# Output projection's convolution rows as a step of their own, and one operand for the convolution norm's colsums

## The chip, the cores and the metric

The kernel runs on one core of a Trainium2 chip. The metric is device time in microseconds of one execution; the time before is the median of three runs. A profiled execution of its own gives the trace from which the rows below are read.

## The reference

One inference step of a two-layer decoder, for a prompt of 512 tokens and 8 sample tokens, which the kernel carries as 520 columns. Everything is fp32.

```
for each of 2 layers:
    x += 0.5 * SwiGLU_1(rmsnorm(x))              # 1024 -> 2816 -> 1024
    z  = rmsnorm(x) @ w_in                       # q,k,v,gate of 4 retention heads; q,k,v of 4 attention heads; 2 x 256 conv
    o_r = rmsnorm(retention(...)) * silu(gate)   # 512 rows
    o_a = sliding-window attention with sinks    # 256 rows
    u   = a * sigmoid(g)                         # 256 channels
    y   = depthwise_conv(u, 31 taps) + b
    o_c = silu(layer_norm(y)) @ pw               # 256 rows
    x += concat(o_r, o_a, o_c) @ w_out           # 1024 rows in, 1024 out
    x += 0.5 * SwiGLU_2(rmsnorm(x))
```

layer_norm takes the mean over the 256 channels, subtracts it, and divides by the root of the mean square of what is left.

## The kernel before, in words

Activations lie with channels on the partitions and the 520 columns along the free dimension: `x` is 8 blocks of 128 channels. Each fp32 operand is split into a high and a low part (`xh`, `xl`; for weights `wh`, `wl`), and `mm3` makes a product of 128 by 128 weights with 520 columns from three pairs of parts, in two halves of 260 columns: six matmuls. Weights come from HBM in chunks of eight such blocks (512 KB), four raw buffers deep. A chunk is split by ScalarE (`split_hi`, the high part) and VectorE (`split_lo`, the low part) into one of three buffers each; a split can only begin when the last matmul on the chunk three before it is done.

Between the two FFNs of a layer lies the mix stage. Its steps are generators, and each `yield` ends a piece of a step. `ORDER`, written out by hand, names the step of which the next piece is issued; each engine then runs its own instructions in that order. The names that matter here:

- `h` and `l` are the next chunk's high and low split; the high split runs on ScalarE (L290), the low one on VectorE (L296).
- `cv` is what follows the convolution's taps (`conv_rest`): a sum over 256 channels by a matmul with a constant matrix (`colsum`, L361), the mean subtracted (L726), the square (L728), another colsum, the reciprocal root, the silu, the split, the product with `pw`, and the split of the result.
- `n0` to `n3` are the retention heads' norms: square (L1140), colsum, three ScalarE and three VectorE instructions. `g0` to `g3` multiply by the gate and split into `xh` and `xl` (L1163 to L1168).
- `s0` to `s3` are the attention of 128 prompt tokens each: scores (L852), row maximum with bias (L837, VectorE), exponentials (L864, ScalarE), reciprocal sum, scaling (L873, ScalarE), transposes (L879), their copy from PSUM (L884, ScalarE), product with the values (L891), its high cast (L899, ScalarE) and low part (L901, VectorE). `sa` is the same for the sample tokens (scores L919).
- `AQ`, `AK`, `AV`, `RG` and others are the input projection's blocks of 128 rows with what follows each; `rs0`, `rs1` update the sample state (L1024, L1026).
- `a0` to `a7` and `b0` to `b7` are the output projection: `a` multiplies the four retention rows of w_out (24 matmuls) for one block of 128 output channels and adds the result to x (L1184); `b` does the same for two attention and two convolution rows (24 matmuls), and after its add issues `prep` for the next FFN: `xh` (L385, ScalarE), `xl` (L387, VectorE), the square (L392), and the sum of squares (`acc`, L395).

PSUM is four tiles of two banks each. A tile is free again when its last reader in the written order is done. Scratch rows (`wt`) rotate through six buffers. The next FFN's first hidden step begins right after `b7`, takes two PSUM tiles at once (gate and up, alternating), reads all eight blocks of `xh` and `xl`, and at its end issues the norm's colsum from `acc`.

Of the kernel before, what the change touches and what calls it, by code (L numbers as in the profile page):

```python
# [87 lines left out]

ORDER = """
CG0 al nrm h nrm pw l nrm pw h nrm l nrm CG0 rd RK0 CG0 CA0 h RK0 l CA1 CA0 h CG0 t l t t t CG1 t h t l t t t t CA1 t  # L90
RV1 h CG1 t CG1 l t t t t RV2 h t t RV1 l t t t t RV3 t RV1 h t RV2 l t t t t t RK1 h l t RV3 RV2 t ts ts RV1 RK1 t h
l RV2 RV1 RK1 RK1 RV2 RQ0 RK1 CG1 t t t t RQ0 t t h t l t t t t RQ1 RV3 RV0 h RQ1 qr l t t t t t RG0 t h t RV0 l t t t
RG0 t t RV0 AQ0 h t RG0 l t t t t AQ1 h AQ0 l t t RV0 h RV3 AQ1 RV3 RV0 t ri2 t AQ1 rv ri0 rv AQ1 RK0 cv ri0 AQ0 AQ0
rl AK0 AQ1 cv ri2 AQ1 rs0 cv RK0 rs0 AQ1 l h rs1 AV0 l rs1 AK0 AK0 RG1 h AK0 AV0 l AV0 rm RG1 h RG1 l AQ0 rm rm cv AQ0
RG2 AQ0 cv qs cv RG3 h RG2 cv l RG2 cv h RG3 AV0 RG3 cv AV0 RK0 kv cv kv cv kv AK0 l AK0 ri2 AK0 AK0 ri0 ri2 s1 ri0 n0
n2 s1 n1 n0 n3 s0 n3 n2 s0 n0 n1 n0 s3 s1 g0 n2 s1 n1 n2 g0 s1 n1 g2 n3 g1 s1 g1 g0 n3 g3 s0 s1 sa s2 g2 s3 g1 g3 s3
s1 s1 g2 g3 s0 s0 s1 sa a0 s3 s3 s2 a1 sa a0 s2 sa a2 a1 h s2 s2 l s3 a2 a3 s3 sa s3 a3 h sa s0 l s3 sa s0 s3 s0 sa s0
s2 a4 s0 s2 a5 a4 a6 a5 sa h s2 a6 a7 s2 s2 b0 l h l b1 b0 b0 b1 b0 b0 b2 h b0 b1 b1 b2 b1 b2 b1 b2 b3 l b4 h b3 b3 l
b2 b3 b5 b4 b3 b2 b4 b3 b4 b6 h b5 b5 l b4 b5 b7 a7 b6 b5 b4 b5 b6 b6 b7 b6 b7 b6 b7 b7 b7
""".split()  # L100


# [1 line left out]
START = "x0 h0 x1 s0 s1 h1 x2 x3 s2 h2 x4 s3 x5 s4 h3 x6 s5 x7 s6 s7 c2".split()  # L104


OUT = dict(a=("R0", "R1", "R2", "R3"), b=("A0", "A1", "C0", "C1"))


def ffn_steps():  # L110
# [14 lines left out]
def streams():  # L125

    w_in = [n for i, n in enumerate(ORDER) if len(n) == 3 and n[:2].isupper() and n not in ORDER[:i]]
    w_out = [(r, int(n[1])) for i, n in enumerate(ORDER) if n[0] in OUT and n[1:].isdigit() and n not in ORDER[:i] for r in OUT[n[0]]]
    return w_in, w_out
# [7 lines left out]
def step_kernel(ctx: ExitStack, tc: tile.TileContext, io: dict):  # L137
    nc = tc.nc
# [25 lines left out]
    ones = {}  # L164
# [13 lines left out]
    def prm(l, name, i=0, n=1):  # L178
        o = P_OFF[name] + i
        return par[:, l, o : o + n]  # L180
# [3 lines left out]
    def v2(t):  # L184
        return t.rearrange("p (a b) -> p a b", a=2)

    def unit(dt=F32):
        return units.tile([128, UNIT], dt, tag="m", name="m")
# [150 lines left out]
    def mm3(o, w, vh, vl, first, last):  # L339
        for i, (a, b) in enumerate(((w[0], vl), (w[0], vh), (w[1], vh))):  # L340
            for s in range(2):
                nc.tensor.matmul(  # L342
                    o[:, s, :HN], lhsT=a, rhs=b[:, s * HN : (s + 1) * HN],
                    start=first and i == 0, stop=last and i == 2,
                )
# [3 lines left out]
    def table(name):  # L349
        if act[0] != name:  # L350
            nc.scalar.preload_act_table_set(name)
            act[0] = name
# [5 lines left out]
    def colsum(o, w, parts):  # L358
        for i, v in enumerate(parts):
            for s in range(2):  # L360
                nc.tensor.matmul(  # L361
                    o[:, s, :HN], lhsT=w, rhs=v[:, s * HN : (s + 1) * HN],
                    start=i == 0, stop=i == len(parts) - 1,
                )
# [5 lines left out]
    def rsqrt(out, o):  # L370

        m = o[:, :, :HN]
        y0, t = wt("y0"), wt("nt")
        table(LNEXP)
        nc.scalar.activation(v2(y0), m, AF.Ln, bias=epst)
        nc.scalar.activation(y0, y0, AF.Exp, scale=-0.5)
        nc.scalar.activation(t, y0, AF.Square, scale=math.sqrt(0.5))
        yield
        nc.vector.scalar_tensor_tensor(v2(t), m, epst[:, :1], v2(t), op0=ALU.add, op1=ALU.mult)
        nc.vector.scalar_tensor_tensor(out, t, 1.5, y0, op0=ALU.subtract, op1=ALU.mult, reverse0=True)  # L380
# [221 lines left out]
    def mix(l, after):  # L602
# [5 lines left out]
        qs = su[:, 48:80].rearrange("p (a b e) -> p a b e", a=2, e=2)  # L608
# [5 lines left out]
        def two(t):  # L614
            return t[:, :UNIT].rearrange("p (c t) -> p c t", c=2)
# [102 lines left out]

        def conv_rest():
            y = conv["y"]  # L720
            o = ptile()
            colsum(o, ones[256], [y[:, 0], y[:, 1]])
            yield
            yc = two(unit())
            for c in range(2):
                nc.vector.tensor_sub(v2(yc[:, c]), v2(y[:, c]), o[:, :, :HN])  # L726
            yield
            nc.scalar.activation(y, yc, AF.Square)  # L728
            yield
            o = ptile()  # L730
            colsum(o, ones[256], [y[:, 0], y[:, 1]])
            yield
            r = wt("lnr")
            yield from rsqrt(r, o)
            for c in range(2):
                nc.vector.tensor_mul(y[:, c], yc[:, c], r)
            yield
            hi, lo = two(unit(F32R)), two(unit(F32R))
            table(SILU)
            for c in range(2):  # L740
                nc.scalar.activation(
                    y[:, c], y[:, c], AF.Silu, scale=prm(l, "ln_g", c), bias=prm(l, "ln_b", c)
                )
                nc.scalar.copy(hi[:, c], y[:, c])
            yield
            for c in range(2):
                nc.vector.tensor_sub(lo[:, c], y[:, c], hi[:, c].bitcast(F32))
            yield
            os = []
            for m in range(2):  # L750
                o = ptile()
                os.append(o)
                for k in range(2):
                    s = slice(k * 256 + m * 128, k * 256 + m * 128 + 128)
                    mm3(o, (pw[0][:, s], pw[1][:, s]), hi[:, k], lo[:, k], k == 0, k == 1)
            yield
            hl = two(unit(F32R)), two(unit(F32R))
            for m, o in enumerate(os):
                nc.scalar.copy(v2(hl[0][:, m]), o[:, :, :HN])
            yield  # L760
            for m, o in enumerate(os):
                nc.vector.tensor_sub(v2(hl[1][:, m]), o[:, :, :HN], v2(hl[0][:, m]).bitcast(F32))
            conv["o"] = hl
            yield
# [299 lines left out]
        def ret_sample_q():  # L1064
            for e in range(2):
                s = slice(64 * e, 64 * e + 64)
                nc.scalar.copy(qs[s, :, :, e], ret["q"][s, :, SEQ:])
            yield
# [103 lines left out]
        def row_input(name):  # L1172
            j = int(name[1])
            if name[0] == "R":
                return ret["hl", j]
            h_, l_ = (att if name[0] == "A" else conv)["o"]
            return h_[:, j], l_[:, j]

        def out(names, m, last):
            o = ptile()  # L1180
            for i, n in enumerate(names):
                mm3(o, next_tile(False), *row_input(n), i == 0, i == len(names) - 1)
            yield
            nc.vector.tensor_add(v2(x[:, m]), v2(x[:, m]), o[:, :, :HN])  # L1184
            yield
            if last:
                yield from after(m)

        def chunk_hi():
            while True:  # L1190
                split_hi()
                yield

        def chunk_lo():
            while True:
                split_lo(1)
                yield

        steps = dict(
            h=chunk_hi(), l=chunk_lo(), nrm=norm(), pw=pw_split(), rd=decayed(), ts=token_scales(), t=conv_taps(),  # L1200
            cv=conv_rest(), al=att_load(), AK0=att_qk(None), AV0=att_v(), qs=att_sample_q(), qr=ret_sample_q(), sa=att_sample(),
            rv=ret_vs(), rl=ret_load(), kv=ret_kv(), rm=ret_sample(), ri0=ret_prompt(0), ri2=ret_prompt(2),
        )
        for i in range(KD):
            steps.update({n + str(i): out(rows, i, n == max(OUT)) for n, rows in OUT.items()})
        for i in range(4):
            steps.update({
                f"RV{i}": ret_v(i), f"RG{i}": ret_gate(i), f"n{i}": ret_norm(i), f"g{i}": ret_out(i),
# [87 lines left out]
def host_arrays(i):  # L1296
# [83 lines left out]
    y=(KD, 128, NT), o_retp=(DEPTH, 4, 64, 128), o_rets=(DEPTH, 2, 128, 1024), o_kp=(DEPTH, 128, 128),  # L1380
# [38 lines left out]
```

## Time and profile before

| | us |
|---|---|
| median of 3 runs | 1912.63 |
| lowest and highest | 1911.82 to 1913.17 |
| the profiled execution's time | 1916.64 |
| its span in the trace | 1914.9 |
| TensorE busy | 1843.5 (96%) |
| VectorE busy | 1565.0 (82%) |
| ScalarE busy | 991.9 (52%) |

The span runs from the first instruction to the last; the execution's time has 1.7 us more around it. Busy is the time in which an engine had an instruction under way. Matmuls overlap each other, so an engine that is busy is not at its peak. In the rows below PE is TensorE, PEld its weight loads, DVE VectorE, ACT ScalarE and SP the engine that issues the loads.

### The profile page before, as it was taken

To read this page: it belongs to the slowest core of one execution; us is meant where nothing else is said; L and a number is where in the kernel's file an instruction comes from. 1 tells how busy PE (TensorE), PEld (TensorE's weight loads), DVE (VectorE), ACT (ScalarE), POOL (GpSimd) and SP (SyncE) were. 2 spreads that over 40 slices of the span, in tenths; PEclk is the share of its full clock that TensorE was granted. 3 is DMA by queue.
4 is the path that set the end of the run, shared out by engine and by line. 5 is a ranking of instruction groups with operands and counts; after the bars stand their busy time and mean duration, and the time that the engine had idled before them with its cause. 6 is when DMAs were issued, how large, how long until landed. Compare 5 with 4: busy or idle time off the path is not lost.

```text
span 1914.9 us, 37060 instructions
## 1 busy us (share of the span) xinstructions
PE 1843.5 (96%) x15182; PEld 1818.6 (95%) x15182; DVE 1565.0 (82%) x2691; ACT 991.9 (52%) x1844; POOL 23.3 (1%) x52
## 2 busy tenths in 40 slices
PE   8999999999989999999999999999998999999998
PEld 8999999999989999999999999999998999999998
DVE  8988898688667989888778988976886579889984
ACT  6545555433765645545455455545237555455452
POOL 0000000000100000000000000000000000000000
PEclk9999999999999999999999999999999999999999
DMA  5233333433313222333333332434332132333332
GB/s 181 77 101 100 89 100 111 138 108 114 117 35 97 79 89 89 90 110 98 112 88 90 91 97 89 123 110 127 100 114 102 45 98 69 100 107 92 93 96 89
DMA packets 54170, 189.35 MB, mean 99 GB/s; under 512 B 6272, under 2 KB 7152, under 8 KB 54000
## 3 DMA queue, kind: packets, MB, share of 16 engines
q1 hardware_dynamic: 50784, 177.35, 30.4%
q0 software_dynamic: 3072, 9.53, 1.5%
q8 instruction: 119, 1.95, 0.4%
q14 instruction: 51, 0.42, 0.1%
q10 hardware_dynamic: 144, 0.11, 0.0%
HBM read 179.50 MB, written 7.45 MB: 98 GB/s over the span
## 4 chain that ended last, share of the span: by engine, by line
PE 61%; DVE 26%; ACT 5%; DMA 4%; issue 4%; SPq 0%; DVEq 0%; ACTq 0%; POOL 0%; POOLq 0%
PE o L342 32%; PE o L334 27%; DVE wl L296 5%; DMA w<-in_w 3%; DVE wh L296 3%; DVE m L474 2%; DVE u L430 2%; DVE m L502 1%; DVE w L260 1%; DVE Rd L263 1%; ACT t L428 1%; DVE t L557 1%; DVE t L556 1%; DVE t L561 1%; DVE u L556 1%
## 5 line engine op out<-in xcount | busy, mean ns | idle before, releaser
L342 PE MATMUL o<-xl,wh 128*128 128x260 f32 x1920 | 389.3, 284 | 6.6 <-DVE xl L387 6.1
L342 PE MATMUL o<-xh,wl 128*128 128x260 f32 x1920 | 387.1, 283 | 1.1 <-DVE wl L296 1.1
L342 PE MATMUL o<-xh,wh 128*128 128x260 f32 x1920 | 386.9, 283 | 0.0
L334 PE MATMUL o<-m,wh 128*128 128x260 f32 x2592 | 350.5, 285 | 23.0 <-DVE t L443 11.3
L334 PE MATMUL o<-m,wl 128*128 128x260 f32 x2592 | 351.7, 285 | 21.3 <-DVE t L443 9.8
L290 ACT CAST wh<-w 128x1024 fp32r<-128x1024 f32 (+1 forms) x318 | 261.1, 821 | 200.8 <-PE o L342 127.7
L334 PEld LDWEIGHTS o<-m,wh 128*128 128x128 f32 x2592 | 327.4, 189 | 27.3 <-issue 12.3
L334 PEld LDWEIGHTS o<-m,wl 128*128 128x128 f32 x2592 | 328.5, 190 | 25.7 <-issue 10.8
L342 PEld LDWEIGHTS o<-xl,wh 128*128 128x128 f32 x1920 | 296.9, 189 | 7.9 <-ACT wh L355 6.1
L342 PEld LDWEIGHTS o<-xh,wl 128*128 128x128 f32 x1920 | 296.6, 189 | 1.3 <-DVE wl L296 1.3
L342 PEld LDWEIGHTS o<-xh,wh 128*128 128x128 f32 x1920 | 296.1, 189 | 0.0
L296 DVE TENSOR_TENSOR wl<-w,wh 128x1024 fp32r<-128x1024 f32 x150 | 183.3, 1222 | 36.1 <-ACT wh L290 32.7
L342 PE MATMUL o<-m,wh 128*128 128x260 f32 x1024 | 164.5, 282 | 4.1 <-DVE m L510 4.1
L342 PEld LDWEIGHTS o<-m,wh 128*128 128x128 f32 x1024 | 140.0, 188 | 5.0 <-DVE m L510 5.0
L290 ACT CAST wl<-w 128x512 fp32r<-128x512 f32 x168 | 103.9, 619 | 35.3 <-PE o L334 21.6
L290 ACT CAST wh<-Rd 128x512 fp32r<-128x512 f32 x126 | 78.3, 621 | 82.5 <-PE o L334 34.5
L290 ACT CAST wl<-Rd 128x512 fp32r<-128x512 f32 x126 | 78.3, 622 | 80.2 <-PE o L334 34.4
L428 ACT ACTIVATE t<-t 128x520 f32<-128x520 f32 x88 | 56.1, 638 | 122.8 <-DVE t L561 103.8
L334 PE MATMUL o<-xh,wh 128*128 128x260 f32 x624 | 115.4, 282 | 0.0
L334 PE MATMUL o<-xh,wl 128*128 128x260 f32 x624 | 115.4, 282 | 0.0
L296 DVE TENSOR_TENSOR wl<-w,wl 128x512 fp32r<-128x512 f32 x168 | 114.9, 684 | 0.0
L296 DVE TENSOR_TENSOR wh<-w,wh 128x512 fp32r<-128x512 f32 x168 | 114.9, 684 | 0.0
(216 smaller groups left out, 2660.0 us busy)
## 6 DMA issues: line engine op xcount, KB each, us to landing
w<-in_w SPq DMA_DIRECT2D x318, 512.0 KB, 3.6
out_y<-x SPq DMA_DIRECT2D x8, 260.0 KB, 2.0
m<-in_cm POOLq DMA_DIRECT2D x4, 512.0 KB, 4.3
m<-in_s_ret SPq DMA_DIRECT2D x4, 512.0 KB, 5.2
m<-sc POOLq DMA_DIRECT2D x8, 256.0 KB, 4.6
out_o_rets<-m POOLq DMA_DIRECT2D x4, 512.0 KB, 3.4
x<-in_x SPq DMA_DIRECT2D x3, 520.0 KB, 6.8
w<-in_w SPq DMA_DIRECT2D x4, 256.0 KB, 5.2
```

The lines of the kernel that those rows point to most:

```text
L260: nc.vector.tensor_sub(a21, a21, a11)
L263: nc.vector.tensor_sub(Rd[:, 0, :PC], a12, Rd[:, 1, :PC])
L290: nc.scalar.copy(spl[u][0], source(u))
L296: nc.vector.tensor_sub(lo, source(u), h.bitcast(F32))
L334: nc.tensor.matmul(o, lhsT=a[:, s], rhs=b, start=first and j == 0 and i == 0, stop=j == JP - 1 and i == 2, skip_group_check=True,)
L342: nc.tensor.matmul(o[:, s, :HN], lhsT=a, rhs=b[:, s * HN : (s + 1) * HN], start=first and i == 0, stop=last and i == 2,)
L428: nc.scalar.activation(t, t, AF.Silu)
L430: nc.vector.tensor_mul(u, u, t)
L474: nc.vector.tensor_sub(tl[:, c], src, th[:, c].bitcast(F32))
L502: nc.vector.tensor_sub(lo, a, h.bitcast(F32))
L556: nc.vector.tensor_add(d[:, HN:], c, v)
L557: nc.vector.tensor_mul(d[:, HN:], d[:, HN:], R[:, HN:])
```

## The change

The output projection is cut into three steps instead of two: `b` keeps the two attention rows, and a new step `c` multiplies the two convolution rows (12 matmuls) and adds its own result to x. `prep` still follows b's add. `c0` stands in the order behind the scores of s1; `c1` to `c4` stand around the softmax of s1, and `c5` to `c7` behind the sample attention's scores. The eight a steps keep their place, b keeps its place with half of its matmuls. Since w_out's blocks are stored in the order of first use, the two chunks with the convolution's rows now come first, and the h and l pieces from the 22nd on (h21 is the first of them) stand elsewhere. In `conv_rest` each colsum gets one operand, the sum of y's two blocks, made by an added VectorE instruction, in place of two operands that TensorE summed.

```diff
 (ORDER, from the retention's last pieces on)
-... kv cv kv cv kv AK0 l AK0 ri2 AK0 AK0 ri0 ri2 s1 ri0 n0
-n2 s1 n1 n0 n3 s0 n3 n2 s0 n0 n1 n0 s3 s1 g0 n2 s1 n1 n2 g0 s1 n1 g2 n3 g1 s1 g1 g0 n3 g3 s0 s1 sa s2 g2 s3 g1 g3 s3
-s1 s1 g2 g3 s0 s0 s1 sa a0 s3 s3 s2 a1 sa a0 s2 sa a2 a1 h s2 s2 l s3 a2 a3 s3 sa s3 a3 h sa s0 l s3 sa s0 s3 s0 sa s0
-s2 a4 s0 s2 a5 a4 a6 a5 sa h s2 a6 a7 s2 s2 b0 l h l b1 b0 b0 b1 b0 b0 b2 h b0 b1 b1 b2 b1 b2 b1 b2 b3 l b4 h b3 b3 l
-b2 b3 b5 b4 b3 b2 b4 b3 b4 b6 h b5 b5 l b4 b5 b7 a7 b6 b5 b4 b5 b6 b6 b7 b6 b7 b6 b7 b7 b7
+... kv cv kv cv kv AK0 l AK0 ri2 AK0 AK0 ri0 ri2 s1 c0 c0 ri0
+n0 n2 s1 n1 n0 n3 s0 n3 n2 s0 n0 n1 n0 s3 s1 g0 n2 s1 n1 n2 g0 c1 c1 s1 n1 c2 c2 g2 c3 c3 n3 h c4 c4 g1 l s1 g1 g0 n3
+g3 s0 s1 sa c5 c5 c6 c6 c7 c7 h s2 l g2 s3 g1 g3 s3 s1 s1 g2 g3 s0 s0 s1 sa a0 s3 s3 s2 a1 h sa a0 s2 l sa a2 a1 s2 s2
+s3 a2 a3 h s3 sa s3 l a3 sa s0 s3 sa s0 s3 s0 sa s0 s2 a4 s0 s2 a5 h a4 a6 a5 l sa s2 a6 a7 h s2 s2 b0 l b1 b0 b0 b1 b0
+b0 b2 b0 b1 b1 b2 b1 b2 b1 b2 b3 h b4 b3 b3 l b2 b3 b5 b4 b3 b2 b4 b3 b4 b6 b5 b5 b4 b5 b7 a7 b6 b5 b4 b5 b6 b6 b7 b6
+b7 b6 b7 b7 b7

-OUT = dict(a=("R0", "R1", "R2", "R3"), b=("A0", "A1", "C0", "C1"))
+OUT = dict(a=("R0", "R1", "R2", "R3"), b=("A0", "A1"), c=("C0", "C1"))

         def conv_rest():
             y = conv["y"]
-            o = ptile()
-            colsum(o, ones[256], [y[:, 0], y[:, 1]])
+            ys = wt("ys")
+            nc.vector.tensor_add(ys, y[:, 0], y[:, 1])
+            o = ptile()
+            colsum(o, ones[256], [ys])
             yield
...
             nc.scalar.activation(y, yc, AF.Square)
-            yield
-            o = ptile()
-            colsum(o, ones[256], [y[:, 0], y[:, 1]])
+            ys = wt("ys")
+            nc.vector.tensor_add(ys, y[:, 0], y[:, 1])
+            yield
+            o = ptile()
+            colsum(o, ones[256], [ys])
             yield
...
-            steps.update({n + str(i): out(rows, i, n == max(OUT)) for n, rows in OUT.items()})
+            steps.update({n + str(i): out(rows, i, n == "b") for n, rows in OUT.items()})
```

## Rows read from the trace of the kernel before

**Rows 1.** The page's part on busy time: us, share of the span, instructions.

```profile
PE 1843.5 (96%) x15182; PEld 1818.6 (95%) x15182; DVE 1565.0 (82%) x2691; ACT 991.9 (52%) x1844; POOL 23.3 (1%) x52
```

**Rows 2.** TensorE's waits over the span: total us, times, longest.

```profile
PE o L334 <- DVE t L443: 21.0, 12, 2.5
...
PE o L879 <- ACT m L873: 9.3, 2, 4.6
...
PE o L361 <- ACT rsq L1140: 1.8, 2, 0.9
PE o L342 <- DVE wl L296: 1.1, 1, 1.1
```

**Rows 3.** Windows of layer 0's chain: us, each engine's busy time, granted clock, DMA share.

```profile
528.00:530.00 2.00, 0.00 (x0) 0.00 (x0) 1.29 (x4) 1.94 (x4) 0.00 (x0) 1.00 0.00 0
...
534.00:536.00 2.00, 2.00 (x11) 1.41 (x10) 2.00 (x5) 1.94 (x4) 0.00 (x0) 0.50 0.03 8
```

**Rows 4.** Timeline of layer 0's chain: start, us, engine, line, operation, idle before.

```profile
529.66 0.76 DVE L379 SCALAR_TENSOR_TENSOR nt<-o,epst,nt 128x520 f32<-128x520 f32 x1 [0.67 <-ACT nt L377]
...
532.52 1.97 PE L879 MATMUL o<-cc,m 128*128 128x128 f32 x8 [4.63 <-ACT m L873]
534.42 3.62 PE L919 MATMUL o<-m 128*32 128x128 f32 x16
...
540.59 0.51 PE L342 MATMUL o<-xl,wh 128*128 128x260 f32 x2 [0.40 <-DVE st L837]
```

**Rows 5.** The chain that ended last, two pieces of layer 0's mix stage.

```profile
478.27 11.54 PE o L342 x96
...
568.10 37.40 PE o L342 x312
```

**Rows 6.** Groups by line and shape (busy us, mean ns), and one timeline row of two adds.

```profile
L296 DVE TENSOR_TENSOR wl<-w,wh 128x1024 fp32r<-128x1024 f32 x150 | 183.3, 1222 | 36.1 <-ACT wh L290 32.7
...
L387 DVE SCALAR_TENSOR_TENSOR xl<-x,par,xh 128x520 fp32r<-128x520 f32 x48 | 36.3, 758 | 20.7 <-ACT xh L385 20.7
...
L395 DVE TENSOR_TENSOR acc<-acc,sq 128x520 f32<-128x520 f32 x42 | 29.2, 695 | 0.7 <-ACT sq L392 0.2
...
L1184 DVE TENSOR_TENSOR x<-x,o 128x520 f32<-128x520 f32 x32 | 22.0, 693 | 25.7 <-PE o L342 25.5
...
591.08 1.30 DVE L1184 TENSOR_TENSOR x<-x,o 128x520 f32<-128x520 f32 x2
```

**Rows 7.** Timeline of layer 0 around cv's two colsums, by engine.

```profile
469.57 2.02 PE L361 MATMUL o<-m,one 128*128 128x260 f32 x8
...
493.64 3.66 PE L361 MATMUL o<-m,one 128*128 128x260 f32 x8
...
471.28 0.16 DVE L964 TENSOR_TENSOR su<-m,R 128x8 f32<-128x8 f32 x1
...
478.03 1.23 DVE L1024 SCALAR_TENSOR_TENSOR m<-m,su 128x1024 f32<-128x1024 f32 x1 [2.13 <-DMA m<-sc]
...
482.69 1.22 DVE L296 TENSOR_TENSOR wl<-w,wh 128x1024 fp32r<-128x1024 f32 x1
...
479.81 1.06 ACT L728 ACTIVATE m<-m 128x1040 f32<-128x1040 f32 x1
```

**Rows 8.** Timeline of layer 0's a steps, ScalarE, VectorE and TensorE.

```profile
550.91 0.99 ACT L884 COPY m<-o 128x1024 f32<-128x1024 f32 x1
553.09 1.06 ACT L290 CAST wh<-w 128x1024 fp32r<-128x1024 f32 x1 [1.19 <-PE o L342]
...
568.14 0.37 ACT L899 CAST m<-o 128x256 fp32r<-128x256 f32 x1 [3.14 <-PE o L891]
570.97 1.05 ACT L290 CAST wh<-w 128x1024 fp32r<-128x1024 f32 x1 [2.45 <-PE o L342]
...
568.54 0.42 DVE L901 TENSOR_TENSOR m<-o,m 128x256 fp32r<-128x256 f32 x1 [0.78 <-ACT m L899]
...
553.39 1.14 PE L891 MATMUL o<-m 128*64 128x128 f32 x16
```

More of the change, by code (lines that the diff above doesn't have):

```diff
@@ L90 @@
 CG0 al nrm h nrm pw l nrm pw h nrm l nrm CG0 rd RK0 CG0 CA0 h RK0 l CA1 CA0 h CG0 t l t t t CG1 t h t l t t t t CA1 t
[L91 to L94, printed above, removed]
@@ L95 @@
-RG2 AQ0 cv qs cv RG3 h RG2 cv l RG2 cv h RG3 AV0 RG3 cv AV0 RK0 kv cv kv cv kv AK0 l AK0 ri2 AK0 AK0 ri0 ri2 s1 ri0 n0
-n2 s1 n1 n0 n3 s0 n3 n2 s0 n0 n1 n0 s3 s1 g0 n2 s1 n1 n2 g0 s1 n1 g2 n3 g1 s1 g1 g0 n3 g3 s0 s1 sa s2 g2 s3 g1 g3 s3
-s1 s1 g2 g3 s0 s0 s1 sa a0 s3 s3 s2 a1 sa a0 s2 sa a2 a1 h s2 s2 l s3 a2 a3 s3 sa s3 a3 h sa s0 l s3 sa s0 s3 s0 sa s0
-s2 a4 s0 s2 a5 a4 a6 a5 sa h s2 a6 a7 s2 s2 b0 l h l b1 b0 b0 b1 b0 b0 b2 h b0 b1 b1 b2 b1 b2 b1 b2 b3 l b4 h b3 b3 l
-b2 b3 b5 b4 b3 b2 b4 b3 b4 b6 h b5 b5 l b4 b5 b7 a7 b6 b5 b4 b5 b6 b6 b7 b6 b7 b6 b7 b7 b7
+RV1 h CG1 t CG1 l t t t t RV2 h t t RV1 l t t t t RV3 t RV1 h t RV2 l t t t t t RK1 h l t RV3 RV2 t ts ts RV1 RK1 t h l
@@ new lines @@
+RV2 RV1 RK1 RK1 RV2 RQ0 RK1 CG1 t t t t RQ0 t t h t l t t t t RQ1 RV3 RV0 h RQ1 qr l t t t t t RG0 t h t RV0 l t t t
+RG0 t t RV0 AQ0 h t RG0 l t t t t AQ1 h AQ0 l t t RV0 h RV3 AQ1 RV3 RV0 t ri2 t AQ1 rv ri0 rv AQ1 RK0 cv ri0 AQ0 AQ0 rl
+AK0 AQ1 cv ri2 AQ1 rs0 cv RK0 rs0 AQ1 l h rs1 AV0 l rs1 AK0 AK0 RG1 h AK0 AV0 l AV0 rm RG1 h RG1 l AQ0 rm rm cv AQ0 RG2
+AQ0 cv qs cv RG3 h RG2 cv l RG2 cv h RG3 AV0 RG3 cv AV0 RK0 kv cv kv cv kv AK0 l AK0 ri2 AK0 AK0 ri0 ri2 s1 c0 c0 ri0
+n0 n2 s1 n1 n0 n3 s0 n3 n2 s0 n0 n1 n0 s3 s1 g0 n2 s1 n1 n2 g0 c1 c1 s1 n1 c2 c2 g2 c3 c3 n3 h c4 c4 g1 l s1 g1 g0 n3
```

## The prediction

> **What bounds the kernel now.** The page first: TensorE is busy 96% of the span of 1914.9 us, VectorE 82% [rows 1]. So the reader looks for what TensorE still waits for. TensorE's own waits come to some 67 us, the longest sum of them (21.0 us, on L443) in the FFN, which the change does not touch [rows 2]. The change sits in the mix stage, and there TensorE waits, per layer, some 4.6 us for the scaled softmax rows (L873, 9.3 us in two waits), 0.9 us for the norm's square (L1140) [rows 2] and 0.4 us ahead of the first a step [rows 4]: 5.9 us a layer. The windows over layer 0's chain show the rest: from 528 us on TensorE does nothing while VectorE and ScalarE work on, and afterwards it runs at a granted clock of 0.50, 1.2 GHz [rows 3]. The transposes and the sample attention issued there take 1.97 + 3.62 us [rows 4], twice what they would at 2.4 GHz, so 2.7 us is the clock's. At most 8.6 us a layer can be filled.
>
> The timeline says who sets the end of the chain. The first a step starts at 540.59 us and waits for VectorE's L837, the row maximum of s3, which frees its PSUM buffer [rows 4]. That is VectorE's queue and not TensorE's. It also says which buffer a new tile takes: of three free ones a0 has the one released first (those of s1 and of the sample attention were released later in the written order). I use that below.
>
> **The change, part by part.** All steps are issued in the written order, on each engine in order.
>
> *The C rows.* The matmuls are the same ones, 12 of a former b step's 24 now in a c step. A stretch of 312 such matmuls takes 37.40 us, 0.12 us each [rows 5], so a c step takes 1.44 us and eight take 11.5 us a layer, which leave the b steps. Eight x adds come new, 693 ns each; two in a row take 1.30 us, so the next starts 0.08 us before the end of the one ahead and an add holds the queue for 0.61 us, a split of 1222 ns for 1.14 [rows 6]. All eight stand ahead of a0 in VectorE's queue, and so do two weight splits (h and l) which were behind it: 8 x 0.61 + 2 x 1.14 = 7.2 us on the queue that sets a0. Then I follow the order. c0's add stands before s1's row maxima and holds them 2 us, but ScalarE is busy with a norm, so the chain loses only 0.4 us. c1 finds no free PSUM buffer until n2's rsqrt has read its sum (L379, today from 529.66 us for 0.76 us [rows 4], then 0.4 us later), at about 530.9 us, so TensorE still idles 2.2 us. VectorE waits for c4, c6 and c7 (0.4, 0.3 and 0.8 us) and, since h of the fifth output chunk needs c7's buffer, 0.5 us for that split; of these 2.0 us some 0.4 fall into time that it idles now. a0 comes 7.2 + 0.4 + 1.6 = 9.2 us later, with 11.5 us of matmuls already done: a gain of 2.3 us a layer. Bounds: a gain of 4.3 (only the 7.2 us) and a loss of 0.5 (twice the waits and c1's stall carried through).
>
> *The clock.* The windows show the granted clock at 0.50 after the idle stretch [rows 3]. With C rows in the gap the clock may stay at 2.4 GHz, but the 2.7 us lie where VectorE sets the end, so I count them at nothing; if that cover were gone they would be worth 5.4 us for both layers. The Trainium skill, "TensorE: Matmul & The Clock Gate" (section "What's actually happening"), has the half rate as the default state and activity as what lifts it; on the fall after idle time the trace agrees, and by the Trainium skill's rule the 5.4 us would be got back.
>
> *The first colsum* (cv, L722). It is 2.02 us for eight records [rows 7]; one operand halves it, 0.97 us less. But its operand is now a VectorE add in the same step, and in VectorE's queue this step stands behind the attention split L789 and L964, of which the second starts at 471.28 us because the first waits for ScalarE. TensorE reached the colsum at 469.57 us. So the add ends at 472.1 us and TensorE waits 2.5 us: +1.55 us a layer, the same in layer 1 by the same order. Below: nothing lost if the queue were early; above: +4.5 if the clock falls after the stall.
>
> *The second sum.* The add waits for the square (479.81 us, 1.06 us), which follows a norm that itself follows TensorE's colsum, now 1.55 us later. On VectorE it stands between the two halves of the sample state (L1024 begins at 478.03), and behind it stand the other half, a rsqrt and the split of RG1's weights (482.69 us) [rows 7]. The square ends at 482.5, the add at 483.2, the state's half at 484.4, the rsqrt and q at 486.6, the split at 487.8; RG1's low part is wanted at 486.1: AV0 and RG1 run from 478.27 us for 11.54 us [rows 5], RG1's half from 484.0, its low part 0.5 us into it, all 1.55 us later. That is a stall of 1.8 us in layer 0. In layer 1 TensorE waits for that split already, 1.1 us [rows 2], and the same steps make it 0.7 us worse. The bounds are 0 and 4 for both layers. The second colsum itself takes 3.66 us at the low clock [rows 7]; half of it, 1.8 us a layer, comes back, or 0.8 if the next matmuls inherit the low clock. Before the chain: 1.55 + 1.8 - 1.8 = +1.6 in layer 0, 1.55 + 0.7 - 1.8 = +0.4 in layer 1 (rounded at the end).
>
> *The splits h, moved.* An h takes the weight buffer of three chunks before, so it waits for the last matmul on that chunk. Now each h stands right behind that last step, so ScalarE is held there with whatever follows. Two places matter. Behind a3's h stands the PSUM copy of s3 (s3, sixth step), and TensorE needs it right after a3. Today the copy runs at 550.91, before that h (553.09, which waited for TensorE), and s3's product starts at 553.39 without a wait [rows 8]. In the new order the copy starts after h, at 554.05, ends at 555.04, and the product starts at 555.15: +1.76 us. Behind a7's h stands the cast of s2's output, which b0 needs; today the cast is at 568.14 and that h at 570.97, again after a wait for TensorE [rows 8]. New: a7's end, h for 0.96 us, cast 0.37, VectorE's subtraction 0.42, with the handovers 1.87 us in which TensorE stands idle. Both a layer, each between 0 and 2.1 us.
>
> *The b steps.* Each now takes 1.44 us on TensorE, but on VectorE still add, xl and acc: 0.61 + 0.67 + 0.7 = 2.0 us, and two weight splits [rows 6]. Eight b steps are 11.5 us on TensorE. The next FFN's first tile needs two PSUM buffers; the first to come free are those of b5 and a7, and a7's add is written behind b5's xl. From b0's start VectorE does one split (rest), six b adds, six xl, three acc, one split and a7's add: 4.3 + 4.0 + 2.2 + 1.1 us (the adds with a7's) plus 1.6 us before b0's first add and 2.3 us of waits on TensorE and ScalarE's casts, so 15.5 us. TensorE wants the second buffer at 11.5 + 0.7 = 12.2 us: +3.4 us a layer. Without those 2.3 us it would be 1.1, with twice as much 5.7. The norm's low part, late by 1.2 us otherwise, fits under that wait. Today b takes 23 us on TensorE and nothing of this shows.
>
> **The sum.** From the chain on, each layer: -2.3 + 1.76 + 1.87 + 3.4 = +4.7. Layer 0: 1.6 + 4.7 = +6.3; layer 1: 0.4 + 4.7 = +5.1; together +11.4 us. On the profiled execution's 1916.64 us (span 1914.9, 1.7 us around it) that is 1928.0; that execution lies 4.0 us above the median of the runs, so I forecast 1912.63 + 11.4 = 1924.0 us, slower by 0.6%.
>
> **Rivals.** (1) *The chain is really filled.* If ScalarE and VectorE take the added instructions in their gaps, TensorE gets all 8.6 us a layer in the chain and not 2.3: 11.4 - 12.6 = -1.2, 1911.4 us, between 1904 and 1917 with the other terms' bounds. For it: the idle stretch and the low clock [rows 3]. Against it: VectorE and ScalarE are busy 2.00 and 1.94 of 2 us in the window from 534 us. It decides from 6.1 us of gain a layer on; below that the change is slower. The Trainium skill's page on the clock gate, named above, stands with this rival. (2) *The moved splits hold nothing*, since ScalarE reaches them late anyway: 7.3 us less, 1916.7 us. Against: [rows 8] show h waiting for TensorE at both places. (3) *The new stalls take the clock down*: the colsum's and the b steps' in each layer, if dense matmuls behind them take twice their time for a stretch as long as the transposes and the sample attention took, 5.6 us, lose 2.8 us each: +5.6 for one a layer, +11.2 for both, 1930 to 1935 us. For it: the fall in [rows 3]; against: it is the only idle stretch of the chain that shows one.
>
> **Chances.** My forecast 0.60 (its own range 1918 to 1929), rival 1 0.22, rival 2 0.10, rival 3 0.08. A change of this kernel within 0.2% (1908.8 to 1916.5 us) is no more than runs can tell from none. Rival 1 gives 0.09 faster, 0.11 same and 0.02 slower; rival 2 0.05 same and 0.05 slower; of the forecast 0.01 is same; the rest is slower: faster 0.09, same 0.17, slower 0.74. The range reaches down into rival 1 and up into rival 3: 1911 to 1931.
>
> **What would show it.** In the changed profile TensorE's wait for ScalarE's L873 should be gone or short, and new waits stand in its list: cv's colsum for VectorE's sum (2.5 us, twice), L296 ahead of RG1 (about 2 us each layer), L891 for ScalarE's L884 (1.8 us), the first b step for VectorE's L901 (1.9 us), and the next FFN's first tile for VectorE's add to x (3.4 us with b7's). a0 should start 9 us later counted from s1's first matmul. I am wrong if the C rows pull a0 to under 6 us, if VectorE's b tail keeps up with 1.44 us a step, or if the buffers are handed out otherwise than first released, first taken.

## The result and the profile after

The changed kernel takes 1927.75 us, median of four runs (1925.34 to 1933.35), against 1912.22 us for the kernel before in four runs beside them: a ratio of 1.0094, interval 1.0077 to 1.0111. It is slower by 0.9%; the forecast was 1924.0 us, the range 1911 to 1931. Its profiled execution takes 1926.78 us, the span 1924.7 us. First the page's part on busy time, as in [rows 1]:

```profile
PE 1837.2 (95%) x15166; PEld 1811.8 (94%) x15166; DVE 1576.4 (82%) x2711; ACT 992.2 (52%) x1844; POOL 23.3 (1%) x52
```

TensorE has 16 matmuls less (four colsums, each with four less) and is busy 6.3 us less, in a span that is 9.8 us longer. VectorE has 20 instructions more. So it is waits that have grown. TensorE's waits over the span, against [rows 2] (total us, times, longest; lines of code are 1 to 5 higher in the changed kernel, up to 12 in the runs below):

```profile
PE o L343 <- DVE x L1189: 6.6, 8, 1.2
PE o L343 <- DVE nt L380: 5.9, 4, 1.9
...
PE o L362 <- DVE ys L723: 5.1, 2, 2.6
...
PE o L343 <- DVE wl L297: 3.3, 2, 1.7
PE o L896 <- ACT m L889: 3.3, 2, 1.6
PE o L343 <- DVE st L842: 3.3, 2, 1.6
PE o L343 <- DVE m L906: 3.3, 2, 1.6
```

The 9.3 us for the scaled rows and the 1.8 us for the norm's square are gone, and seven kinds of wait have come or grown (those for L297 and L842 were 1.1 and 0.4 us), 30.8 us in all, nearly all on VectorE. They are in layer 0's timeline of TensorE in the order in which they come (the bracket: idle before, and what ended it):

```profile
468.80 1.52 PE L362 MATMUL o<-ys,one 128*128 128x260 f32 x4 [2.56 <-DVE ys L723]
...
486.09 0.51 PE L343 MATMUL o<-xh,wl 128*128 128x260 f32 x2 [1.67 <-DVE wl L297]
...
529.98 0.74 PE L343 MATMUL o<-m,wh 128*128 128x260 f32 x4 [1.88 <-DVE nt L380]
...
533.06 1.23 PE L343 MATMUL o<-m,wh 128*128 128x260 f32 x4 [0.79 <-DVE x L1189]
...
539.53 1.04 PE L884 MATMUL o<-cc,m 128*128 128x128 f32 x8
540.53 1.91 PE L924 MATMUL o<-m 128*32 128x128 f32 x16
...
543.51 0.75 PE L343 MATMUL o<-m,wh 128*128 128x260 f32 x4 [1.07 <-DVE nt L380]
...
551.87 0.51 PE L343 MATMUL o<-xl,wh 128*128 128x260 f32 x2 [1.62 <-DVE st L842]
...
566.37 1.15 PE L896 MATMUL o<-m 128*64 128x128 f32 x16 [1.63 <-ACT m L889]
...
585.78 0.75 PE L343 MATMUL o<-m,wh 128*128 128x260 f32 x4 [1.62 <-DVE m L906]
...
596.45 0.74 PE L343 MATMUL o<-m,wh 128*128 128x260 f32 x4 [0.33 <-DVE x L1189]
...
599.14 0.51 PE L343 MATMUL o<-xl,wh 128*128 128x260 f32 x2 [0.99 <-DVE x L1189]
...
601.31 0.51 PE L343 MATMUL o<-xl,wh 128*128 128x260 f32 x2 [1.18 <-DVE x L1189]
```

They are the colsum that waits for the sum, RG1's low split, c1, c2 and c5 for a PSUM tile, a0, s3's product behind a3, b0, and the tail: a b step and the next FFN's first two tiles. The two rows without a bracket are the transposes and the sample attention, which took 1.97 and 3.62 us before [rows 4]. ScalarE's and VectorE's rows show how such a wait is made:

```profile
467.26 0.70 DVE L794 TENSOR_TENSOR m<-asq,m 128x520 fp32r<-128x520 f32 x1 [1.87 <-ACT m L792]
467.88 0.16 DVE L969 TENSOR_TENSOR su<-m,R 128x8 f32<-128x8 f32 x1
467.96 0.69 DVE L723 TENSOR_TENSOR ys<-m 128x520 f32<-128x520 f32 x1
...
564.36 1.04 ACT L291 CAST wh<-w 128x1024 fp32r<-128x1024 f32 x1 [0.69 <-PE o L343]
565.31 1.01 ACT L889 COPY m<-o 128x1024 f32<-128x1024 f32 x1
```

The sum (L723) stands behind a split that waits 1.87 us for ScalarE, though y itself was ready (its last writer, L717, ended at 465.4 us); and the copy of s3 stands behind the high split h, which waited for TensorE's a3. Both as the prediction placed them.

There is one thing more. Windows of the changed kernel, of layer 0 behind the first colsum and in the chain (the number before the last two is the granted clock):

```profile
470.00:472.00 2.00, 2.00 (x10) 1.90 (x10) 2.00 (x4) 0.00 (x0) 1.92 (x4) 0.50 0.40 117
...
532.00:534.00 2.00, 1.21 (x6) 0.94 (x5) 1.66 (x3) 1.97 (x5) 0.00 (x0) 0.50 0.00 0
534.00:536.00 2.00, 2.00 (x11) 2.00 (x10) 1.17 (x2) 1.07 (x2) 0.00 (x0) 0.50 0.01 4
```

Behind the 2.56 us wait dense matmuls run at 1.2 GHz, and so do c2 and c3 behind c1's and c2's waits.

**A ledger by pieces.** For what follows I cut each layer's mix stage at four starts on TensorE: the transpose of the sample's values (L1004, 464.86 us in layer 0 of the changed kernel), s1's scores (519.44), a0 (551.87), b0 (585.78) and the norm's colsum (612.20). The pieces are called pre, chain, a and tail. They repeat to 0.05 us between executions unless the clock differs, whereas the rest of the span, mostly FFNs, which nobody changed, takes 1629.4 to 1637.7 us in these executions. That is why the mix stages below differ by 16.4 us where the two spans above differ by 9.8: the execution before has the longest rest of all. Layer 0 / layer 1, us; the last column is the sum of both layers, and e9 and e12 are second executions of the changed kernel and of the kernel before.

| | pre | chain | a | tail | sum |
|---|---|---|---|---|---|
| before | 51.92 / 54.86 | 20.41 / 20.40 | 30.42 / 30.43 | 34.33 / 34.37 | 277.14 |
| before (e12) | 51.90 / 54.56 | 20.41 / 20.40 | 30.41 / 30.42 | 34.33 / 34.37 | 276.80 |
| changed | 54.58 / 56.11 | 32.43 / 29.78 | 33.91 / 33.92 | 26.42 / 26.43 | 293.58 |
| changed (e9) | 54.55 / 54.53 | 32.40 / 32.43 | 33.90 / 33.93 | 26.43 / 26.42 | 294.59 |
| e1 | 53.48 / 54.81 | 29.79 / 32.44 | 33.92 / 33.91 | 26.41 / 26.42 | 291.18 |
| e2 | 57.76 / 59.06 | 20.40 / 20.39 | 30.43 / 30.42 | 34.33 / 34.38 | 287.17 |
| e3 | 57.74 / 57.77 | 29.77 / 29.80 | 30.42 / 30.43 | 26.56 / 26.57 | 289.06 |
| e4 | 54.52 / 59.01 | 32.40 / 29.79 | 33.92 / 33.92 | 24.26 / 24.27 | 292.09 |
| e5 | 54.56 / 54.52 | 30.38 / 30.42 | 33.91 / 38.65 | 27.77 / 26.40 | 296.61 |
| e10 (e5 again) | 53.01 / 54.55 | 30.40 / 27.76 | 33.89 / 38.65 | 27.72 / 26.42 | 292.40 |
| e6 | 49.15 / 54.32 | 20.41 / 20.40 | 30.41 / 30.43 | 34.32 / 34.37 | 273.81 |
| e7 | 50.84 / 52.04 | 27.73 / 27.76 | 30.80 / 30.82 | 22.95 / 22.91 | 265.85 |
| e11 (e7 again) | 50.57 / 54.02 | 27.72 / 27.75 | 30.80 / 30.82 | 22.96 / 22.91 | 267.55 |
| e8 | 50.54 / 54.31 | 22.82 / 22.80 | 30.41 / 30.42 | 28.75 / 28.60 | 268.65 |

The 96 matmuls of a layer's C rows (11.52 us, as in [rows 5]) have gone from the tail to the chain: to compare with the kernel before, read its chain as 31.93 us and its tail as 22.81.

### The profile page after: what moved, and what is told of

It is laid out like the page before. It is cut to its first block, busy times and chain, and to the rows that moved or that the text cites. A ratio compares the mean times of both kernels' runs of the same rounds, so it can differ in the third digit from the quotient of the medians.

```text
span 1924.7 us, 37051 instructions
## 1 busy us (share of the span) xinstructions
PE 1837.2 (95%) x15166; PEld 1811.8 (94%) x15166; DVE 1576.4 (82%) x2711; ACT 992.2 (52%) x1844; POOL 23.3 (1%) x52
## 4 chain that ended last, share of the span: by engine, by line
PE 60%; DVE 27%; ACT 5%; issue 4%; DMA 3%; SPq 0%; DVEq 0%; ACTq 0%
PE o L343 32%; PE o L335 26%; DVE wl L297 5%; DVE wh L297 3%; DMA w<-in_w 3%; DVE u L431 2%; DVE m L475 2%; DVE m L503 1%; DVE w L261 1%; DVE Rd L264 1%; ACT t L429 1%; DVE t L558 1%; ACT wh L291 1%; DVE t L557 1%; DVE t L562 1%
## 5 line engine op out<-in xcount | busy, mean ns | idle before, releaser
L297 DVE TENSOR_TENSOR wl<-w,wh 128x1024 fp32r<-128x1024 f32 x150 | 183.1, 1222 | 34.0 <-ACT wh L291 30.5
L297 DVE TENSOR_TENSOR wl<-w,wl 128x512 fp32r<-128x512 f32 x168 | 114.9, 684 | 0.0
L297 DVE TENSOR_TENSOR wh<-w,wh 128x512 fp32r<-128x512 f32 x168 | 114.9, 684 | 0.0
```

The costliest lines, as they stand in the source:

```text
L297: nc.vector.tensor_sub(lo, source(u), h.bitcast(F32))
```

## The experiments

Ratios are against the kernel before, which ran on the same chip: 1909.66 us there for e1 to e4, 1911.30 us for e5 to e8. e9 to e12 are single executions.

**e1, two operands.** The changed kernel, its convolution norm as before.

```diff
-            ys = wt("ys")
-            nc.vector.tensor_add(ys, y[:, 0], y[:, 1])
             o = ptile()
-            colsum(o, ones[256], [ys])
+            colsum(o, ones[256], [y[:, 0], y[:, 1]])
```
(both sums)

> The changed kernel with both colsums on two operands again (c steps and order as changed). The two traces put the piece from the retention's scores to s1's first matmul 2.7 us (layer 0) and 1.25 us (layer 1) later than before, and TensorE waits 2.56 us for the added sum twice. Theory (the sums stand too late in VectorE's queue): both vanish, 3.9 us less than the changed kernel, so 12 to 13 us over the kernel before, and the two waits are gone. Rival (the colsum's half that is saved pays for the stall, the loss is all in the output projection): no difference, 16 to 17 us over the kernel before.

Measured: 1926.51 us, 1.0082 (1.0058 to 1.0106): some 16 us over the kernel before, as the rival has it, though the interval reaches from 11 to 20 us and does not refute the theory's 12 to 13. The pieces show the theory's part: the waits for the sum and for layer 0's RG1 are gone, layer 1's is 1.0 us as before, and no half clock follows the first colsum. Pre is 2.4 us shorter than the changed kernel's over both layers. Chain, a and tail are those of the changed kernel. The C rows alone, 1.0082 of 1.0094, make most of the loss.

**e2, one operand only.** The kernel before with the sums of the change and nothing else.

```diff
+            ys = wt("ys")
+            nc.vector.tensor_add(ys, y[:, 0], y[:, 1])
             o = ptile()
-            colsum(o, ones[256], [y[:, 0], y[:, 1]])
+            colsum(o, ones[256], [ys])
```
(both sums)

> The kernel before with one operand for each colsum and nothing else. Theory: two waits of 2.5 us for the sum and a longer wait for RG1's low split, minus half of two colsums a layer: 3 to 5 us slower than before. Rival (the adds are hidden, only the halves count): 1.0 + 1.8 us a layer come back, 5 us faster than before.

Measured: 1916.61 us, 1.0033 (1.0018 to 1.0049). TensorE waits 2.56 us for the sum and 1.67 us for RG1's split in each layer. That is 7 us slower, somewhat over the 3 to 5 expected: even with nothing else changed, the sums cost more than the halved colsums give back. In this execution the clock fell behind the second colsum as well, which is why pre is 3 us longer than in the changed kernel under the same waits.

**e3, two splits later.** The changed kernel; the high splits behind a3 and a7 stand one piece later, behind s3's copy and s2's cast.

```diff
-... a3 h s3 sa s3 l a3 ... a7 h s2 s2 b0
+... a3 s3 h sa s3 l a3 ... a7 s2 h s2 b0
```

> The changed kernel with two of the h pieces one place later in the order: the one behind a3 now stands behind s3's copy from PSUM, the one behind a7 behind s2's high cast. Theory: ScalarE's held queue is what TensorE waits for at both places (1.63 us each in the trace, 3.5 us a layer with what follows), so 7 us less than the changed kernel and both waits gone. Rival (the chain is late anyway, the wait moves to the next step): at most 2 us less.

Measured: 1922.71 us, 1.0066 (1.0045 to 1.0086). The waits on L889 and L906 are gone from the list, and a is 30.42 us in both layers, to 0.01 us that of before: 7.0 us less than in the changed kernel over both layers, as expected (the medians differ by 5.0). The whole of the 3.5 us a layer in the a steps is the place of these two splits.

**e4, a7's add early.** The changed kernel; a7's add to x stands behind b0's matmuls and not behind b7's.

```diff
-... s2 s2 b0 l b1 ... b4 b5 b7 a7 b6
+... s2 s2 b0 a7 l b1 ... b4 b5 b7 b6
```

> The changed kernel with a7's add to x written right behind b0's matmuls and not behind b7's, so that its PSUM buffer is free for the b steps. Theory: the next FFN's second buffer is then free with b5's add, about 13.3 us after b0's start and not 15.5; the waits of 0.33, 0.99 and 1.18 us shrink to about 1 us in all, 2.3 us a layer and 4 to 5 us less than the changed kernel. Rival (VectorE's work as such bounds the tail): the wait moves to the norm's colsum for its low part, 0 to 1 us less.

Measured: 1923.70 us, 1.0066 (1.0044 to 1.0089). One wait of 0.9 us is left of the three in the tail, which is 2.2 us shorter in each layer and still 1.5 us longer than 22.81. This is 4 us less than the changed kernel, as expected. Most of the tail's stall is a PSUM tile that stands full because its reader is late on VectorE; the rest is gone in e7, where b5's add stands earlier too.

**e5, chain splits.** The changed kernel; three weight splits stand later.

```diff
-... c3 c3 n3 h c4 c4 g1 l s1 ... c7 c7 h s2 l g2 s3 g1 g3 s3 s1 ... a0 s3 s3 s2 a1
+... c3 c3 n3 h c4 c4 g1 s1 ... c7 c7 s2 g2 s3 g1 g3 s3 h s1 ... a0 s3 l s3 s2 l a1
```

> The changed kernel with three weight splits of the chain written later: the low split of the sixth output chunk behind s3's reciprocal, the next high split behind s3's exponentials, the next low split behind s2's row maxima. Everything else is as changed. Theory (VectorE's and ScalarE's queues set the first a step, and each split ahead of it holds them): two splits of 1.14 us leave the queue, and one hold of a high split with them, so the first a step comes 2.3 to 3.5 us earlier a layer and the whole takes 5 to 7 us less than the changed kernel, 0.25 to 0.35%. Rival (TensorE's own work, at the half clock, sets the chain once the convolution rows are in it): 0 to 2 us less.

Measured: 1928.86 us, 1.0106 (1.0088 to 1.0125): not the expected gain, and not faster than the changed kernel. But the waits ahead of c5 and of a0 have shrunk from 1.07 and 1.62 us to 0.22 and 0.26, and at the same clock the chain is 2.0 us shorter: 30.38 to 30.42 us against 32.40 to 32.43 with half clock in it. Elsewhere the ledger shows layer 1's a piece at 38.65 us and layer 0's tail at 27.77. Layer 1 behind s3's product, a row of TensorE's timeline and four windows:

```profile
1520.58 3.41 PE L947 MATMUL o<-m 128*128 128x4 f32 x16
```

```profile
1520.00:1522.00 2.00, 2.00 (x12) 2.00 (x10) 0.42 (x1) 0.79 (x2) 0.00 (x0) 0.50 0.75 252
1522.00:1524.00 2.00, 2.00 (x12) 1.98 (x13) 0.00 (x0) 0.00 (x0) 0.00 (x0) 0.50 0.00 0
1524.00:1526.00 2.00, 2.00 (x13) 1.67 (x14) 0.42 (x1) 0.70 (x3) 0.00 (x0) 0.50 0.00 0
1526.00:1528.00 2.00, 2.00 (x11) 2.00 (x10) 0.00 (x0) 1.01 (x1) 0.00 (x0) 0.50 0.00 0
```

TensorE is busy 2.00 of 2 us in each and runs at half clock all the same, some 10 us long; what it is busy with are small matmuls, 16 of them with four columns. Against the changed kernel this costs 38.65 - 33.92 = 4.7 us, the tail 1.35 us, so 6.1 us lost for 2 x 2.0 gained; set against the changed kernel's second execution, which has half clock in both chains as e5 has, that is the whole difference (296.61 against 294.59).

**e6, sums placed.** The kernel before with one operand, each sum a piece of its own, put where VectorE idles.

```diff
-... t ri2 t AQ1 rv ... rs1 AK0 AK0 RG1 h
+... t ri2 t cv AQ1 rv ... rs1 AK0 cv AK0 RG1 h
             nc.vector.tensor_add(ys, y[:, 0], y[:, 1])
+            yield
             o = ptile()
```
(the yield after both sums)

> The kernel before with one operand for the colsums alone, as in e2, but each of the two adds is a piece of its own, so that the order can place it: the first right behind the last tap, the second right behind AK0's scaling, where VectorE idles. Theory (the loss in e2 is that the adds stand behind other work in VectorE's queue, and the half clock that follows the wait): no wait for the sum and none for RG1's split; half of each colsum, 1.0 and 1.8 us, comes back in each layer, so 5 to 6 us less than the kernel before, 0.3%, and 11 to 13 us less than e2. Rival 1 (the half clock follows the colsums with or without the wait): 1 to 3 us less than before. Rival 2 (the adds cost by their time on VectorE wherever they stand): not faster than before.

Measured: 1909.23 us, 0.9993 (0.9980 to 1.0007), no difference from the kernel before where 5 to 6 us less were expected, and 7 us less than e2 where 11 to 13 were. TensorE's list has no wait for the sum, and none for layer 0's RG1; layer 1's grew from 1.1 to 1.9 us:

```profile
PE o L342 <- DVE wl L296: 1.9, 1, 1.9
```

Pre is 2.8 us shorter in layer 0, where no half clock follows the second colsum now, and 0.5 in layer 1, where half clock stood for 3.4 us behind RG1's wait of 1.9 us and for 3.4 us more behind the second colsum. So the pieces give the sums 3.3 us in this execution, of which the clock has a part; that is near the first rival's 1 to 3 us, and the times do not tell it from nothing. What they are worth hangs on their place: from 1.0033 to 0.9993, some 7 us, by two instructions moved.

**e7, all four.** The changed kernel with e6's sums, e5's splits, e3's splits, e4's a7 and b5's add right behind b4's.

```diff
-... b3 b3 l b2 b3 b5 b4 b3 b2 b4 b3 b4 b6 b5 b5 b4 b5
+... b3 b3 l b2 b3 b5 b4 b5 b3 b2 b4 b3 b4 b6 b5 b4 b5
```
(and the diffs of e3 to e6)

> The changed kernel with the four causes taken away together: both sums placed as in e6, the chain's splits as in e5, the two high splits behind the last a steps' neighbours as in e3, and a7's add to x as early as in e4, with b5's right behind b4's. Theory (the causes are separate, and add up): of a layer the part before the chain 2.7 us shorter than before, the chain 1 to 3 us, the a steps as before, the tail 0 to 0.5 us longer, so 7 to 11 us less than the kernel before, 0.35 to 0.6%. Rival (VectorE, with eight more adds of 0.61 us a layer and 82% busy, gives each wait that is taken away back at the next place): between the changed kernel and the kernel before.

Measured: 1902.58 us, 0.9959 (0.9945 to 0.9973), faster than both kernels. From its list of TensorE's waits, the four largest of the mix stage:

```profile
PE o L343 <- DVE nt L380: 3.7, 2, 1.9
PE o L343 <- DVE x L1191: 1.6, 2, 0.8
PE o L343 <- DVE wl L297: 1.3, 1, 1.3
PE o L898 <- ACT m L891: 0.6, 2, 0.3
```

The chain takes 27.73 and 27.76 us, 4.2 less than 31.93; a is 0.4 longer, the tail 0.1, and pre 1.1 and 2.8 shorter. The whole, 8.7 us less, is as expected; of its terms the chain gave more than the 1 to 3 us expected and pre less than 2.7. The chain's 4.2 us are the 2.0 us of e5's splits and the 2.1 us that the changed kernel has in the layer where the clock stayed: the C rows in the chain are worth having once the queue ahead of a0 is short and the clock stays up.

**e8, four c.** As e7, but with only c0 to c3 in the chain; b4 to b7 keep four rows.

```diff
+NC = 4
+def out_rows(n, m):
+    return OUT[n] + (OUT["c"] if n == "b" and m >= NC else ())
...
-            steps.update({n + str(i): out(rows, i, n == "b") for n, rows in OUT.items()})
+            steps.update({n + str(i): out(out_rows(n, i), i, n == "b") for n in OUT})
```
(in the order no c4 to c7, no split of the output's weights ahead of a0; sums and a7 as in e7)

> A half measure: only the first four output blocks have a convolution step in the chain (c0 to c3), b4 to b7 keep their four rows as in the kernel before, no weight split stands in the chain, and the sums and a7's add are placed as in e7. So four adds more a layer in place of eight, 5.8 us of matmuls in the chain in place of 11.5, and the last four b steps last 2.9 us on TensorE. Theory (each add holds the chain by 0.61 us and each convolution step fills it by 1.44 us, the tail is VectorE's only where the b steps are short): no wait in the tail, the chain 3 us shorter than before by the same matmuls, so 10 to 11 us less than the kernel before, 0.5 to 0.6%. Rival (what pays in the chain is the number of matmuls in it): 3 to 4 us more than e7.

Measured: 1903.97 us, 0.9967 (0.9957 to 0.9978): 7.3 us less than the kernel before, short of the 10 to 11 expected. The chain is 22.8 us against 20.41 + 5.76, a gain of 3.4 us; the tail of 28.75 and 28.60 stands against 34.33 - 5.76. The first four C steps give 3.4 of the 4.2 us that e7's eight give. It takes 1.4 us more than e7, where the rival has 3 to 4; the two kernels' intervals overlap, and which is better is not settled.

**e9 to e12, second executions.** Four kernels again, to see what the clock does under the same instructions.

> The changed kernel as it is, for a second profiled execution. Theory (the wait for the first sum takes TensorE's clock down each time, whereas in the chain the clock falls or not from one execution to the next under the same waits): the same waits to 0.1 us; the half clock behind the first colsum in both layers; in the chain the piece from s1's scores to the first a step takes 29.8 us where the clock stays and 32.4 us where it falls, in either layer. Rival (the layer decides): layer 0 again 32.4 us, layer 1 again 29.8 us.

Measured: 1927.94 us. The waits are the same. Layer 1's chain takes 32.43 us and has the half clock that it lacked the first time. The changed kernel's first execution, and then its second:

```profile
1491.00:1493.00 2.00, 2.00 (x19) 2.00 (x18) 1.97 (x4) 1.65 (x3) 0.00 (x0) 1.00 0.00 0
```

```profile
1490.00:1492.00 2.00, 2.00 (x11) 2.00 (x11) 1.11 (x3) 1.50 (x3) 0.00 (x0) 0.50 0.00 0
```

The same c steps: 19 matmuls in 2 us, and 11. So it is not the layer that decides. How the half clock reaches a0 shows on VectorE, in the adds of c1 to c4 in the changed kernel's first execution, first layer 0, with half clock, then layer 1, without:

```profile
532.31 0.70 DVE L1189 TENSOR_TENSOR x<-x,o 128x520 f32<-128x520 f32 x1 [0.85 <-PE o L343]
...
536.06 0.70 DVE L1189 TENSOR_TENSOR x<-x,o 128x520 f32<-128x520 f32 x1 [0.86 <-PE o L343]
...
538.29 0.70 DVE L1189 TENSOR_TENSOR x<-x,o 128x520 f32<-128x520 f32 x1 [0.92 <-PE o L343]
539.73 0.70 DVE L1189 TENSOR_TENSOR x<-x,o 128x520 f32<-128x520 f32 x1 [0.75 <-PE o L343]
```

```profile
1489.32 0.70 DVE L1189 TENSOR_TENSOR x<-x,o 128x520 f32<-128x520 f32 x1 [0.27 <-PE o L343]
...
1492.13 0.69 DVE L1189 TENSOR_TENSOR x<-x,o 128x520 f32<-128x520 f32 x1
...
1493.35 0.69 DVE L1189 TENSOR_TENSOR x<-x,o 128x520 f32<-128x520 f32 x1
1494.68 0.70 DVE L1189 TENSOR_TENSOR x<-x,o 128x520 f32<-128x520 f32 x1 [0.64 <-PE o L343]
```

VectorE waits 3.4 us for them in the one and 0.9 us in the other; in layer 1 of the second execution, with half clock, it waits 0.27, 0.85, 1.29 and 0.95 us.

> e5's kernel once more. Theory (e5 gained 2.05 us a layer in the chain by VectorE's queue and lost it to the clock, which stood at half rate for 34 us of the two mix stages where the changed kernel had 17): the same waits, the chain at 27.7 us where the clock stays and 30.4 us where it falls, and the part of the a steps back at 33.9 us unless the clock falls there again. Rival (the a steps of layer 1 took 38.7 us in e5 because of the order): 38.7 us again in layer 1.

Measured: 1928.40 us. Layer 1's chain is 27.76 us without half clock, as expected. But its a piece is 38.65 us again, and layer 0's tail 27.72: the rival was right there, these two falls came in both executions of this kernel and in no other one. And layer 0 shows the wait for the sum without a fall behind it:

```profile
471.00:473.00 2.00, 2.00 (x19) 2.00 (x18) 2.00 (x4) 0.00 (x0) 1.85 (x4) 1.00 0.47 154
```

Its pre is 53.01 us against 54.55: one such fall costs 1.5 us, and 2.8 in the layer 1 of e2 and of e4, where it stood for 7 us and not 3.4.

> e7's kernel once more. Theory (with fewer waits ahead of the chain and in it the clock stays up there): no half clock in the chain in either layer, 27.7 us each, and one short stretch behind the second colsum. Rival (e7 had luck): a fall in the chain of one layer at least, 30.4 us there.

Measured: 1901.42 us, both chains without half clock again, 27.72 and 27.75 us. It stood for 3.4 us around the second colsum in each layer, and in layer 1 for 3.4 us more behind RG1's wait of 1.85 us.

> The kernel before as it is. Theory (its idle stretch of 4.6 us in the chain takes the clock down each time): half clock in the chain of both layers and the chain at 20.4 us with or without a longer one, since VectorE sets its end; the part before the chain between 49 and 58 us by the clock behind the second colsum. Rival (the clock in the chain varies there too): no fall in one layer.

Measured: 1911.43 us, half clock in the chain of both layers for 7 us, as in the first execution. The rival falls.

## Why the prediction was right, and where its sum was off

The direction, the mechanism and most sizes held. The forecast, by its own terms, and the second executions (e9 less e12, whose times differ by 16.5 us and whose pieces by 17.8):

| term, us a layer | forecast | measured |
|---|---|---|
| before the chain, layer 0 / 1 | +1.6 / +0.4 | +2.65 / -0.03 |
| chain | -2.3 | +0.5 (-2.1 where the clock stays up, in the first execution's layer 1) |
| h behind a3 and a7 | +1.76 and +1.87 | +3.5 together |
| tail | +3.4 | +3.6 |
| both layers | +11.4 | +17.8 |

- **The waits.** The first colsum's was put at 2.5 us and is 2.56; RG1's at 1.8 and is 1.67; c1's at 2.2 and is 1.88; s3's at 1.76 and is 1.63; b0's at 1.87 and is 1.62. e3 shows that the last two are the splits' places, e6 that the first two are the sums'. The queue model, which counts what stands ahead in each engine's written order, carried all five. The profiled execution, put at 1928.0 us and measured at 1926.78, is near by luck: outside the mix stages it took 6.6 us less than the profiled execution before, which the mix stages' extra loss makes up for.
- **The first colsum and the clock.** The sum took the wait less the matmuls saved, +1.55, and left the fall to the upper bound. The fall came in 12 of the 14 layers that have this wait (changed, e2 to e5, e9, e10), and in none of the 14 without it (before, e1, e6 to e8, e11, e12). It costs 1.5 us. This is rival 3's mechanism at one of its two places; behind the b steps it came in e5's kernel alone, in layer 0, at a cost of 1.35 us. The second colsum hides part of this: half clock stood there in both layers of e12 and in neither of e9, so more came back than the 1.8 us of the sum (3.66 us before [rows 7], 1.12 in layer 0 of the changed kernel). Layer 1's -0.03 for +0.4 is thus two misses that cancel.
- **The chain: the step that failed.** That a0 comes 9.2 us later held where the clock stays: 29.78 - 20.40 = 9.4 us. But the term "I count them at nothing", since VectorE sets the end, was wrong. With C rows in the chain VectorE's adds wait for c1 to c4, 3.4 us at half clock and 0.9 without (e9), so a slow TensorE delays a0 by VectorE's queue: most of the 32.43 - 29.78 = 2.65 us between the two chains. The clock fell there in 8 of the 14 layers of the changed kernel and its near variants (changed, e1, e3 to e5, e9, e10). In the kernel before it was hidden as the prediction says: in e2 and in layer 1 of e6 half clock stood in the same chain for 3.4 us and not 7, and the chain took 20.39 to 20.40 us all the same. That cover is gone with the change itself, and half clock ate the gain of 2.1 us. In e9, against e12, it did so in both layers: 5.3 of the 6.4 us by which the sum is short.
- **The moved splits ahead of a0.** They were counted at 2 x 1.14 us on VectorE's queue; e5 shows 2.0 us a layer for the three that it moves. What the prediction did not see is that c2 and c5 wait as well, 0.79 and 1.07 us, for tiles that VectorE has not read yet.
- **The tail.** One stall of 3.4 us was forecast, at the FFN's second tile; it is three, 2.5 us together, and the piece is 3.6 us longer, since a wait costs more than its bracket: pairs of matmuls that start 0.24 us apart start 0.73, 1.39 and 1.57 us apart at these three, 3.0 us lost. e4 shows the cause of most of it, a7's late add; that buffers are taken in the order in which they came free fits all of these waits, and no run changes it.
- **Rival 1** (a filled chain) failed by its own deciding point: the gain is 2.1 us a layer at best, not 6.1. What it hoped for needs the queue cleared: e7 has 4.2. The Trainium skill's rule that stood beside it, in "TensorE: Matmul & The Clock Gate", section "What's actually happening", agrees with the transposes and the sample attention, which ran at full clock in all 20 layers profiled with C rows ahead of them (1.04 and 1.91 us); but the 5.4 us were not got back, for in 8 of the 20 the C rows themselves ran at half clock, and where they did not the changed kernel's chain gained 2.1 us and no more. The same section of the Trainium skill says that the chip judges activity in stretches that run on by themselves and do not begin with a kernel; that the same waits gave both outcomes agrees with it, and no run here tests it.
- **Rival 2** (the splits hold nothing) is refuted by e3, where the two splits moved are worth 3.5 us a layer.

What stays open: why the clock never fell in the chain of e7, e8 and e11 (six layers), which have c1's and c2's waits of 1.87 and 0.79 us as the changed kernel has (e7's chain is written as e5's, where it fell in three layers of four), and why it fell in the a steps of e5's kernel alone. The waits that the profile shows don't decide it.

## What to carry to other kernels

To fill one engine's gap, look at the queue that ends the gap: here every C step brought 1.44 us of matmuls into TensorE's idle time and 0.61 us of add into VectorE's full queue, with weight splits moved ahead of a0 on top. That gained 2.1 us a layer, lost again when the clock fell, and 4.2 with those splits taken out and the clock up. An operand that is made by another engine stands where its queue puts it: the same two adds cost 7 us behind a waiting split and nothing that the times show where VectorE idled. When work is moved along a hand-written order, ask of each instruction that moved with it (a split, a copy, an add that frees a buffer) what stands right behind it; such places, and the falls of the clock that came with them, were worth the 25 us between the changed kernel and e7.

## What the runs showed of the hardware

- TensorE's waits alone do not decide the granted clock: the same instructions with the same waits to 0.1 us gave half clock in one execution and full clock in the next (1.00 and 0.50 in the windows above), at 2.65 us a time in the chain and 1.5 us behind the first colsum (3.4 us at half clock there).
- TensorE can run at half clock while it is busy 2.00 of 2 us, some 10 us long in e5: 4.7 us lost with a single wait of 1.63 us ahead of it and then small matmuls (16 and 4 of 128 columns) up to the fall, and 16 of four columns behind it (3.41 us).
- Around the second colsum of a layer, four or eight matmuls behind 32 of two columns, half clock stood in 20 of the 28 layers profiled, with one operand and with two. With two the eight matmuls took 3.66 us there [rows 7], against the first colsum's 2.02; with one the four took 1.62 us in e7's layer 0, against 1.12 in the changed kernel's, where the clock stayed.
- Between dense matmuls on both sides, RG1's wait in layer 1 was followed by half clock at 1.91 us (e6) and 1.85 us (e11) and not at 1.92 us (e8).
